# Strassen-like down projection of an MLP on one core: weight sums formed in place, a seventh buffer of split weights, first-step weights ahead of the last four u tiles, relu and square on ScalarE

## The chip, the cores and the metric

The kernel runs on one core of one Trainium2 chip. Its time is the device time of one execution in microseconds (us); before the change it is 2210.37 us, the median of three runs (2208.81, 2210.37, 2213.05). Engines are named as the profile names them: PE is TensorE (matmuls), PEld its weight load, DVE VectorE, ACT ScalarE, POOL GpSimd, SP SyncE, which issues the loads.

## The reference, cut to what matters

Two layers, 256 tokens, model width 2048, hidden width 8192, everything in float32. The change touches the MLP, the last line of a layer.

```python
for l in range(DEPTH):
    h = rmsnorm(x, attn_norm[l])
    proj = h @ w_in[l]
    ...                                     # latent attention (a) and retention (r)
    x = x + mixed @ w_o[l]
    h = rmsnorm(x, mlp_norm[l])
    x = x + jnp.square(jax.nn.relu(h @ w_up[l])) @ w_down[l]
return rmsnorm(x, final_norm)
```

## The kernel before, in words

**Weights.** All weights come as float32 from DRAM, one load per piece (`w_load`, L124, on SP's queue), into five raw buffers (N_RAW) of 4 KB a partition. Each raw piece is split into a rounded head, cast on ACT (L189), and a tail, raw minus head, on DVE (L190); head and tail stand in one of six `w` buffers (N_SPLIT). A product with a split operand is then two matmuls: 512 columns (weight head times activation head and tail, `mac_feat`, L223) and 256 columns (weight tail times activation head, L224). These two are called a pair below. `proj_feat` runs one output tile or four of them in PSUM banks of their own, and `join` (an ACT copy, L241, and a DVE add, L242) brings a bank's two halves together.

**The MLP.** A layer's hidden width is worked off in four blocks of 2048 (FB). A block first makes 16 tiles u0 to u15 of squared-relu activations, in four groups of four tiles: four PSUM banks a group, eight in all. Of each tile, join gives t; then t = max(t, 0) * t in one DVE instruction (L759), t times the row scale `rs2b` (L760), and the split into u, head on ACT (L182) and tail on DVE (L183). Each pair of tiles gives a step's combined activations f0 to f7 (`first_factors`, L684 to L687).

The down projection of a block has two parts. Columns 0 to 767 of w_down go through eight steps of `seven_products`: seven products of 3 matmuls of 384 columns each (L724), a Strassen-like scheme of 2 by 2 tiles that keeps seven PSUM banks over the whole block. Its weight operands come from `second_factors`: two loads of 128x768, casts of w11 alone (384 columns) and of w21 and w22 together (768), then four DVE adds into two further buffers of the raw pool (L707, L708, L710, L711), which are cast and split in their turn (768 each). The other columns are done as ordinary tiles: behind nearly every step stands `next_tile` (two loads of 128x8x128, 16 pairs, a join, and an add into x, L777). In a layer's last block a tile stands behind six of the eight steps, and every finished tile goes on into the next norm (`done_x`: L185, L186, L266, L267). A block ends with `gather_products`, which takes the seven banks into SBUF (ACT copies in a layer's first block, DVE adds, L732, in the others). A layer ends with `join_products` (DVE, L738) and the tiles left.

**Order.** The program is built in the order of the Python code, and a scheduler then fixes one order for each engine. Each engine works its own list in order: an instruction that waits holds up what stands behind it on the same engine. The eighth PSUM bank is the only one free while the seven product banks are held, and the raw and `w` buffers are handed round in order.

Of the kernel before, what the change touches and what calls it, by code (L numbers as in the profile page):

```python
# [11 lines left out]
F32 = mybir.dt.float32  # L12
# [28 lines left out]
N_RAW, N_SPLIT = 5, 6  # L41
# [52 lines left out]
def kernel(ctx: ExitStack, tc: tile.TileContext, xt, positions, w_in, w_uq, w_ukv, w_o, w_up, w_down,  # L94
# [35 lines left out]
    for j in range(0, KD, 2):  # L130
# [4 lines left out]
        if j == 8:  # L135
            cst = cpool.tile([P, C_W], F32, name="cst")
            nc.sync.dma_start(cst, consts)
            posi = cpool.tile([P, T], I32, name="posi")
            nc.sync.dma_start(posi, positions.to_broadcast([P, T]))
# [12 lines left out]
    angles = cpool.tile([P, 2, 2, T], F32, tag="tabs", name="angles")  # L152
    turn = cpool.tile([P, T], F32, tag="rsb", name="turn")
    ang, part, k2 = tab[:, 0, 0, :], tab[:, 0, 1, :], tab[:, 1, 0, :]
    ks = [k2, turn, k2]
    nc.gpsimd.tensor_copy(turn, posi)
    nc.gpsimd.tensor_scalar_mul(ang, turn, cst[:, C_FREQ:C_FREQ + 1])
    for k, (turns, parts) in zip(ks, REDUCTIONS):
        nc.gpsimd.tensor_scalar(k, ang, 1.0 / (2 * math.pi * turns), ROUND, op0=ALU.mult, op1=ALU.add)
        for n, size in parts:  # L160
            nc.gpsimd.tensor_scalar(part, ks[n], -ROUND, size, op0=ALU.add, op1=ALU.mult)
            nc.gpsimd.tensor_tensor(ang, ang, part, op=ALU.subtract)
    nc.gpsimd.tensor_scalar(ang, ang, PI_LOW, -PI_LOW, op0=ALU.min, op1=ALU.max)
    for i in range(2):
        nc.gpsimd.tensor_copy(angles[0:64, i, 0, :], ang[i * 64:i * 64 + 64, :])
        nc.gpsimd.tensor_scalar_mul(angles[64:128, i, 0, :], ang[i * 64:i * 64 + 64, :], -1.0)

    def rotary_tables():
        for i in range(2):
            ang, half = angles[:, i, 0, :], angles[:, i, 1, :]  # L170
# [141 lines left out]
    def spread(c, tag=None):  # L312
# [6 lines left out]
        d = cpool.tile([P, T], F32, tag=tag, name=tag)  # L319
# [25 lines left out]
    for l in range(DEPTH):  # L345
        g0 = l * G_LAYER

        with tc.tile_pool(name=f"mix{l}", bufs=1) as ap:
            mixed = [None] * 16

# [40 lines left out]
            def scale_rows():  # L391
# [16 lines left out]
                rows["rsb"] = spread(rows["rs"], "rsb")  # L408
                rows["tkvb"] = spread(rows["tkv"], "tkvb")
                rows["tabs"] = tabs = cpool.tile([P, 2, 2, T], F32, tag="tabs", name="tabs")  # L410
# [195 lines left out]
            def mix_latent():  # L606
# [5 lines left out]
                ta = spread(rc, "tab_a")  # L612
# [36 lines left out]
        with tc.tile_pool(name=f"mlp{l}", bufs=1) as up:  # L649
# [195 lines left out]
```

## Time and profile before

| | |
|---|---|
| runs | 2208.81, 2210.37, 2213.05 us |
| profiled execution | 2210.41 us, span 2208.6 us |
| PE busy | 2159.2 us, 98% of the span |
| DVE busy | 1794.2 us, 81% |
| ACT busy | 1219.0 us, 55% |
| mixer and w_o, layer 1 | to about 355 us |
| eight-step stages, first matmul of L724 | 471.3, 649.9, 827.9, 1005.3 us (layer 1); 1559.9, 1738.5, 1916.1, 2094.8 us (layer 2) |
| eight-step stages, last matmul of L724 | 543.5, 721.7, 899.1, 1074.9 us; 1632.1, 1809.9, 1988.5, 2164.8 us |

A busy share of PE counts matmuls whose ends are modelled, so the pace is better read from the starts of successive matmuls. In a list of instructions each row gives start, busy time, engine, line, operation, and in brackets the idle time of the engine just before it with what ended it.

### The profile page before, as it was taken

Reading aid. Unit: us, or ns where it says so; the run is one execution under the profiler, and the core shown is the slowest. Engines: PE = TensorE matmul, PEld = TensorE weight load, DVE = VectorE, ACT = ScalarE, POOL = GpSimd, SP = SyncE. Lnnn points to the kernel's source line nnn. Section 1 sums busy time; section 2 is a strip of 40 time slices with the busy share of each in tenths; the row PEclk is TensorE's granted clock in tenths of the full one; section 3 lists DMA queues with packets and bytes.
Section 4 is the critical chain, followed back from the end, with each engine's and each line's share of the span. In section 5 each row is a group of like instructions: output and inputs, shape, how many; then the busy total and the mean of one; then the engine's idle time right before and its main releaser. Section 6 shows DMA issues by size and latency. Waiting matters only on the chain.

```text
span 2208.6 us, 33675 instructions
## 1 busy us (share of the span) xinstructions
PE 2159.2 (98%) x12398; PEld 1910.3 (86%) x12398; DVE 1794.2 (81%) x3451; ACT 1219.0 (55%) x1976; POOL 24.5 (1%) x34
## 2 busy tenths in 40 slices
PE   7999999999999999999999999999999999999997
PEld 6888888888888888888898888888888898888876
DVE  8878967788688779788978888668887887887787
ACT  7555546556555555555655554555565555555554
POOL 4000000000000000000000000000000000000000
PEclk9999999999999999999999999999999999999999
DMA  7555556547737755854765555565586476467454
GB/s 244 167 157 177 161 190 186 179 137 218 220 123 201 233 166 168 251 158 148 219 177 154 176 164 168 179 196 167 147 250 188 127 229 210 133 194 236 152 168 128
DMA packets 367845, 400.15 MB, mean 181 GB/s; under 512 B 13120, under 2 KB 271296, under 8 KB 367680
## 3 DMA queue, kind: packets, MB, share of 16 engines
q1 hardware_dynamic: 366720, 397.08, 59.9%
q8 instruction: 97, 1.59, 0.3%
q10 hardware_dynamic: 960, 0.92, 0.1%
q14 instruction: 68, 0.56, 0.1%
HBM read 395.85 MB, written 2.10 MB: 180 GB/s over the span
## 4 chain that ended last, share of the span: by engine, by line
PE 78%; DVE 12%; DMA 6%; ACT 2%; issue 1%; SPq 0%; ACTq 0%; DVEq 0%
PE mm L223 42%; PE mm L224 22%; DMA raw<-w_down 6%; DVE w L190 5%; PE mm L228 3%; PE mm L724 3%; ACT w L189 2%; PE mm L229 1%; PE at L223 1%; DVE raw L708 1%; PE at L224 1%; DVE t L242 1%; DVE raw L710 1%; DVE raw L707 1%; PE at L492 0%
## 5 line engine op out<-in xcount | busy, mean ns | idle before, releaser
L190 DVE TENSOR_TENSOR w<-raw,w 128x1024 fp32r<-128x1024 f32 (+5 forms) x952 | 1014.9, 1077 | 324.9 <-ACT w L189 320.0
L189 ACT CAST w<-raw 128x1024 fp32r<-128x1024 f32 (+5 forms) x952 | 877.7, 933 | 666.7 <-PE mm L224 420.2
L223 PE MATMUL mm<-xs,w 128*128 128x512 f32 x2944 | 1032.6, 394 | 7.7 <-ACT w L189 7.7
L224 PE MATMUL mm<-xs,w 128*128 128x256 f32 x2944 | 826.9, 281 | 4.9 <-DVE w L190 4.9
L223 PEld LDWEIGHTS mm<-xs,w 128*128 128x128 f32 x2944 | 553.2, 188 | 126.4 <-ACT w L189 8.0
L224 PEld LDWEIGHTS mm<-xs,w 128*128 128x128 f32 x2944 | 555.1, 189 | 7.4 <-DVE w L190 7.1
L223 PE MATMUL mm<-u,w 128*128 128x512 f32 x1280 | 452.5, 393 | 5.8 <-ACT w L189 5.8
L224 PE MATMUL mm<-u,w 128*128 128x256 f32 x1280 | 365.5, 286 | 7.7 <-DVE w L190 7.6
L223 PEld LDWEIGHTS mm<-u,w 128*128 128x128 f32 x1280 | 241.7, 189 | 54.8 <-ACT w L189 6.9
L224 PEld LDWEIGHTS mm<-u,w 128*128 128x128 f32 x1280 | 242.5, 189 | 21.5 <-DVE w L190 21.0
L223 PE MATMUL mm<-mix,w 128*128 128x512 f32 x512 | 178.0, 391 | 0.0
L241 ACT COPY tb<-mm 128x256 f32<-128x256 f32 x296 | 106.4, 372 | 122.1 <-PE mm L224 118.2
L724 PE MATMUL mm<-w,f 128*128 128x384 f32 x768 | 155.3, 342 | 4.4 <-ACT w L189 2.5
L724 PEld LDWEIGHTS mm<-w,f 128*128 128x128 f32 x768 | 132.1, 188 | 15.6 <-DVE w L190 7.3
L224 PE MATMUL mm<-mix,w 128*128 128x256 f32 x512 | 143.7, 281 | 0.0
L242 DVE TENSOR_TENSOR t<-mm,tb 128x256 f32<-128x256 f32 x296 | 116.9, 417 | 29.9 <-ACT tb L241 28.9
L724 PE MATMUL mm<-w,u 128*128 128x384 f32 x576 | 127.7, 340 | 9.1 <-DVE t L242 7.6
L223 PEld LDWEIGHTS mm<-mix,w 128*128 128x128 f32 x512 | 96.1, 188 | 20.8
L724 PEld LDWEIGHTS mm<-w,u 128*128 128x128 f32 x576 | 98.8, 188 | 17.1 <-issue 9.9
L182 ACT CAST f<-t 128x256 fp32r<-128x256 f32 x128 | 52.1, 407 | 83.3 <-DVE t L687 44.4
L224 PEld LDWEIGHTS mm<-mix,w 128*128 128x128 f32 x512 | 96.4, 188 | 0.0
L228 PE MATMUL mm<-w,xs 128*128 128x512 f32 x256 | 92.8, 401 | 0.0
(196 smaller groups left out, 1716.0 us busy)
## 6 DMA issues: line engine op xcount, KB each, us to landing
raw<-w_up SPq DMA_DIRECT2D x256, 512.0 KB, 4.5
raw<-w_down SPq DMA_DIRECT2D x160, 512.0 KB, 4.2
raw<-w_in SPq DMA_DIRECT2D x144, 512.0 KB, 4.5
raw<-w_down SPq DMA_DIRECT2D x128, 384.0 KB, 4.9
raw<-w_o SPq DMA_DIRECT2D x64, 512.0 KB, 4.5
raw<-w_uq SPq DMA_DIRECT2D x16, 384.0 KB, 4.1
raw<-w_in SPq DMA_DIRECT2D x16, 320.0 KB, 3.3
raw<-w_ukv SPq DMA_DIRECT2D x8, 512.0 KB, 4.3
```

Source lines behind the costliest of these rows:

```text
L182: nc.scalar.copy(head, src)
L189: nc.scalar.copy(dst_h, src)
L190: nc.vector.tensor_tensor(dst_l, src, dst_h.bitcast(F32), op=ALU.subtract)
L223: nc.tensor.matmul(ps, wk[:, 0, n0:n0 + P], act.rearrange("p s t -> p (s t)"), start=first, stop=False)
L224: nc.tensor.matmul(ps[:, 0:T], wk[:, 1, n0:n0 + P], act[:, 0, :], start=False, stop=last)
L228: nc.tensor.matmul(ps, act[:, 0, t0:t0 + P], wk, start=first, stop=False)
L229: nc.tensor.matmul(ps[:, 0:256], act[:, 1, t0:t0 + P], wk[:, 0], start=False, stop=last)
L241: nc.scalar.copy(tb, ps[:, T:2 * T])
L242: nc.vector.tensor_tensor(dst, ps[:, 0:T], tb, op=ALU.add)
L707: nc.vector.tensor_tensor(sums[0][:, 0, :], w11, w12, op=ALU.add)
L708: nc.vector.tensor_tensor(sums[0][:, 1, :], w22, w12, op=ALU.add)
L724: nc.tensor.matmul(ps[i], a[:, p, :], w[:, q, :], start=first and n == 0, stop=last and n == 2)
```

## The change

Five edits, of which the core of the diff follows. (1) `second_factors` forms its four sums in the two raw buffers themselves, after the casts of w11, w21 and w22 have been taken from them, and so takes two buffers of the raw pool a step instead of four; the last two of its operands change places. (2) There are seven `w` buffers instead of six. Room for it comes from moving some rotary and row-scale tiles into a pool that is open only during the mixer (not shown). (3) In every block the weights of the first step are called for before the joins of the last four u tiles; of these tiles, join and relu come for all four, and the rest (square, row scale, split) stands in the code behind the first step's products, f6 and f7 behind the first two tiles. (4) Relu and square are two ACT instructions in place of one on DVE. (5) At the end of a layer one tile is called for between `gather_products` and `join_products`.

```diff
-N_RAW, N_SPLIT = 5, 6
+N_RAW, N_SPLIT = 5, 7
...
                 parts([w11], w11)
                 parts([w21, w22], raws[1])
-                sums = [wpool.tile([P, 2, SB], F32, tag="raw", name="raw", bufs=N_RAW) for _ in range(2)]
-                nc.vector.tensor_tensor(sums[0][:, 0, :], w11, w12, op=ALU.add)
-                nc.vector.tensor_tensor(sums[0][:, 1, :], w22, w12, op=ALU.add)
-                parts("13", sums[0].rearrange("p i c -> p (i c)"))
-                nc.vector.tensor_tensor(sums[1][:, 0, :], sums[0][:, 0, :], w22, op=ALU.add)
-                nc.vector.tensor_tensor(sums[1][:, 1, :], sums[1][:, 0, :], w21, op=ALU.add)
-                parts("24", sums[1].rearrange("p i c -> p (i c)"))
+                for dst, other in ((w11, w12), (w12, w22), (w22, w11), (w21, w22)):
+                    nc.vector.tensor_tensor(dst, dst, other, op=ALU.add)
+                parts([w11, w12], raws[0])
+                parts([w21, w22], raws[1])
...
-                        join(ps, t)
-                        nc.vector.scalar_tensor_tensor(t, t, 0.0, t, op0=ALU.max, op1=ALU.mult)
-                        nc.vector.tensor_tensor(t, t, rows["rs2b"], op=ALU.mult)
...
+                def next_u(t):
+                    nc.scalar.activation(t, t, AF.Square)
+                    nc.vector.tensor_tensor(t, t, rows["rs2b"], op=ALU.mult)
...
+                def relu_sum(ps):
+                    t = tmp()
+                    join(ps, t)
+                    nc.scalar.activation(t, t, AF.Relu)
+                    return t
...
+                factors = second_factors(b * FB)
+                late = [relu_sum(ps) for ps in pss]
...
-                for k, f in enumerate(fs):
-                    seven_products(pp, us, f, k, b * FB + 2 * k * P, k == 0, k == len(fs) - 1)
+                steps = FB // (2 * P)
+                for k in range(steps):
+                    if k:
+                        factors = second_factors(b * FB + 2 * k * P)
+                    seven_products(pp, us, fs[k], k, factors, k == 0, k == steps - 1)
+                    while late:
+                        next_u(late.pop(0))
                     if k in (LAST_TILE_AFTER if end else TILE_AFTER):
                         next_tile()
+                    if pair:
+                        next_f()
                 gather_products(pp, sums, b == 0)
                 if end:
+                    next_tile()
                     blocks = join_products(sums)
```

Where the change moves instructions, the scheduled lists show. On ACT, where the first block's up phase passes into its steps, the list before reads as follows; `tb` are the copies of the last four u tiles' banks, `w` of 384 and 768 columns belong to step weights and those of 8x128 to a tile.

```order
L189 CAST w_5121<-raw_5117 128x384
L182 CAST f5_4869<-t_4871 128x256
L189 CAST w_5124<-raw_5119 128x768
L189 CAST w_5131<-raw_5127 128x768
L189 CAST w_5136<-raw_5128 128x768
L189 CAST w_5163<-raw_5161 128x8x128
L241 COPY tb_5053<-mm_4880 128x256
L241 COPY tb_5062<-mm_4881 128x256
L241 COPY tb_5082<-mm_4882 128x256
L241 COPY tb_5091<-mm_4883 128x256
L189 CAST w_5184<-raw_5182 128x8x128
L189 CAST w_5212<-raw_5208 128x384
```

The same place on ACT now, from the last copies of the banks on:

```order
L246 COPY tb_5100<-mm_4895 128x256
L776 ACTIVATE t_5089<-t_5089 128x256
L776 ACTIVATE t_5094<-t_5094 128x256
L776 ACTIVATE t_5099<-t_5099 128x256
L762 ACTIVATE t_5084<-t_5084 128x256
L762 ACTIVATE t_5089<-t_5089 128x256
L762 ACTIVATE t_5094<-t_5094 128x256
L187 CAST u12_5134<-t_5084 128x256
L187 CAST u13_5139<-t_5089 128x256
L187 CAST u14_5144<-t_5094 128x256
L762 ACTIVATE t_5099<-t_5099 128x256
L194 CAST w_5215<-raw_5211 128x384
```

The first step's weight casts stood ahead of the four bank copies already and still do; the cast of the first tile's second half has moved ahead of the copies too. New behind the copies are relu (L776) and square (L762) of four tiles. The second step's first two weight casts (w_5215, and w_5218 right behind it) stand ahead of the cast of u15.

On DVE at the same place, before, from the join of tile 12 on (the L190 row is the tail of the first tile's second half, L685 to L687 belong to f6):

```order
L242 TENSOR_TENSOR t_5052<-mm_4880,tb_5053 128x256
L242 TENSOR_TENSOR t_5061<-mm_4881,tb_5062 128x256
L759 SCALAR_TENSOR_TENSOR t_5052<-t_5052 128x256
L759 SCALAR_TENSOR_TENSOR t_5061<-t_5061 128x256
L760 TENSOR_TENSOR t_5052<-t_5052,rs2b_4276 128x256
L760 TENSOR_TENSOR t_5061<-t_5061,rs2b_4276 128x256
L685 TENSOR_TENSOR t_5071<-t_5052 128x128
L684 TENSOR_TENSOR t_5071<-t_5052,t_5061 128x128
L190 TENSOR_TENSOR w_5184<-raw_5182,w_5184 128x8x128
L183 TENSOR_TENSOR u12_5058<-t_5052,u12_5058 128x256
L183 TENSOR_TENSOR u13_5067<-t_5061,u13_5067 128x256
L686 TENSOR_TENSOR t_5072<-t_5071,t_5052 128x128
```

The same place on DVE now, from the tail of the first tile's second half on:

```order
L195 TENSOR_TENSOR w_5176<-raw_5174,w_5176 128x8x128
L247 TENSOR_TENSOR t_5084<-mm_4892,tb_5085 128x256
L247 TENSOR_TENSOR t_5089<-mm_4893,tb_5090 128x256
L247 TENSOR_TENSOR t_5094<-mm_4894,tb_5095 128x256
L247 TENSOR_TENSOR t_5099<-mm_4895,tb_5100 128x256
L763 TENSOR_TENSOR t_5084<-t_5084,rs2b_4276 128x256
L763 TENSOR_TENSOR t_5089<-t_5089,rs2b_4276 128x256
L763 TENSOR_TENSOR t_5094<-t_5094,rs2b_4276 128x256
L188 TENSOR_TENSOR u12_5134<-t_5084,u12_5134 128x256
L188 TENSOR_TENSOR u13_5139<-t_5089,u13_5139 128x256
L188 TENSOR_TENSOR u14_5144<-t_5094,u14_5144 128x256
L763 TENSOR_TENSOR t_5099<-t_5099,rs2b_4276 128x256
```

Before, twelve instructions (the ten rows above from the first L759 on, and two more) stood between the first two joins and the last two; now the four joins follow one another, the weight tail stands ahead of them, and f6 has gone behind the first tile.

On DVE at the end of the first layer, before (L732 are the gathers, L738 the joining of products, w_11081 and w_11102 the halves of the next tile's weights):

```order
L732 TENSOR_TENSOR p6_5855<-p6_5855,mm_10396 128x384
L732 TENSOR_TENSOR p4_5857<-p4_5857,mm_10397 128x384
L738 TENSOR_TENSOR p2_5847<-p1_5845,p2_5847 128x384
L738 TENSOR_TENSOR p6_5855<-p1_5845,p6_5855 128x384
L190 TENSOR_TENSOR w_11081<-raw_11079,w_11081 128x8x128
L738 TENSOR_TENSOR p7_5853<-p6_5855,p7_5853 128x384
L190 TENSOR_TENSOR w_11102<-raw_11100,w_11102 128x8x128
L738 TENSOR_TENSOR p4_5857<-p7_5853,p4_5857 128x384
```

The same place now:

```order
L737 TENSOR_TENSOR p6_5855<-p6_5855,mm_10390 128x384
L737 TENSOR_TENSOR p4_5857<-p4_5857,mm_10391 128x384
L195 TENSOR_TENSOR w_11074<-raw_11072,w_11074 128x8x128
L195 TENSOR_TENSOR w_11095<-raw_11093,w_11095 128x8x128
L743 TENSOR_TENSOR p2_5847<-p1_5845,p2_5847 128x384
L743 TENSOR_TENSOR p6_5855<-p1_5845,p6_5855 128x384
L195 TENSOR_TENSOR w_11135<-raw_11133,w_11135 128x8x128
L743 TENSOR_TENSOR p7_5853<-p6_5855,p7_5853 128x384
```

The next tile's two tails have moved ahead of two and three joining adds, and are still behind the seven gathers.

## Rows read from the trace of the kernel before

**Rows 1.** Page, part 1: busy us (share of span) xinstructions.
```profile
PE 2159.2 (98%) x12398; PEld 1910.3 (86%) x12398; DVE 1794.2 (81%) x3451; ACT 1219.0 (55%) x1976; POOL 24.5 (1%) x34
```

**Rows 2.** Busy time by window: PE, PEld, DVE, ACT, POOL, then clock, DMA share.
```profile
400.00:420.00 20.00, 20.00 (x118) 17.64 (x117) 16.62 (x36) 11.88 (x20) 0.00 (x0) 1.00 0.56 168
460.00:480.00 20.00, 18.87 (x108) 16.60 (x107) 16.56 (x39) 9.54 (x18) 0.00 (x0) 1.00 0.39 118
```

**Rows 3.** Matmuls of L724 in block 1 and block 4 of layer 1.
```profile
L724 PE MATMUL mm<-w,u x72: 333/338/440, 471.3 to 543.5; 128*128 128x384 f32 x72
...
L724 PE MATMUL mm<-w,u x72: 334/337/448, 1005.3 to 1074.9; 128*128 128x384 f32 x72
```

**Rows 4.** PE's instructions in order, start of block 1's first step.
```profile
471.31 1.21 PE L724 MATMUL mm<-w,u 128*128 128x384 f32 x6
472.36 2.24 PE L724 MATMUL mm<-w,f 128*128 128x384 f32 x12
474.44 0.34 PE L724 MATMUL mm<-w,u 128*128 128x384 f32 x1
474.96 0.44 PE L724 MATMUL mm<-w,u 128*128 128x384 f32 x1 [0.18 <-ACT w L189]
475.23 0.34 PE L724 MATMUL mm<-w,f 128*128 128x384 f32 x1
476.52 0.76 PE L724 MATMUL mm<-w,u 128*128 128x384 f32 x3 [0.95 <-DVE t L242]
```

**Rows 5.** DVE's instructions in order, the same stretch of block 1.
```profile
475.96 0.74 DVE L242 TENSOR_TENSOR t<-mm,tb 128x256 f32<-128x256 f32 x2
...
476.96 0.75 DVE L759 SCALAR_TENSOR_TENSOR t<-t 128x256 f32<-128x256 f32 x2
```

**Rows 6.** PE's instructions in order, second step and its tile.
```profile
486.35 0.39 PE L223 MATMUL mm<-u,w 128*128 128x512 f32 x1
487.01 0.39 PE L224 MATMUL mm<-u,w 128*128 128x256 f32 x1 [0.28 <-DVE w L190]
487.24 0.39 PE L223 MATMUL mm<-u,w 128*128 128x512 f32 x1
...
487.58 0.39 PE L223 MATMUL mm<-u,w 128*128 128x512 f32 x1
```

**Rows 7.** ACT's waits, steps of block 1, 500 to 540 us: us, times, longest.
```profile
ACT w L189 <- DMA raw<-w_down: 9.5, 10, 2.0
```

**Rows 8.** Busy time by window, block 4 of layer 1 (columns as in Rows 2).
```profile
1005.28:1075.23 69.95, 65.74 (x363) 57.98 (x361) 65.23 (x118) 42.26 (x68) 0.00 (x0) 1.00 0.56 163
```

**Rows 9.** PE's instructions in order, end of block 1.
```profile
543.71 0.40 PE L223 MATMUL mm<-u,w 128*128 128x512 f32 x1
544.54 0.39 PE L224 MATMUL mm<-u,w 128*128 128x256 f32 x1 [0.43 <-DVE w L190]
```

**Rows 10.** PE's instructions in order, end of layer 1's steps.
```profile
1075.07 0.40 PE L223 MATMUL mm<-u,w 128*128 128x512 f32 x1
1078.63 0.50 PE L223 MATMUL mm<-u,w 128*128 128x512 f32 x1 [3.17 <-ACT w L189]
1080.13 0.58 PE L224 MATMUL mm<-u,w 128*128 128x256 f32 x1 [1.00 <-DVE w L190]
...
1083.49 0.39 PE L223 MATMUL mm<-u,w 128*128 128x512 f32 x1
```

**Rows 11.** ACT's instructions in order, end of layer 1's steps.
```profile
1077.53 1.04 ACT L189 CAST w<-raw 128x1024 fp32r<-128x1024 f32 x1 [0.78 <-DMA raw<-w_down]
```

**Rows 12.** PE's instructions in order, end of layer 2's steps.
```profile
2164.95 0.40 PE L223 MATMUL mm<-u,w 128*128 128x512 f32 x1
2167.63 0.50 PE L223 MATMUL mm<-u,w 128*128 128x512 f32 x1 [2.28 <-ACT w L189]
```

**Rows 13.** ACT's instructions in order, block 1's last four tiles.
```profile
470.47 1.41 ACT L241 COPY tb<-mm 128x256 f32<-128x256 f32 x4 [0.64 <-PE mm L224]
```

**Rows 14.** Groups of ACT instructions: count | busy us, mean ns | idle before.
```profile
L266 ACT ACTIVATE sq<-x 128x256 f32<-128x256 f32 x74 | 29.4, 406 | 10.7 <-DVE ssq L267 6.7 <-DVE x L777 3.9
```

More of the change, by code (lines that the diff above doesn't have):

```diff
@@ L137 @@
             nc.sync.dma_start(cst, consts)
-            posi = cpool.tile([P, T], I32, name="posi")
+            posi = cpool.tile([P, T], I32, tag="rs2b", name="posi")
             nc.sync.dma_start(posi, positions.to_broadcast([P, T]))
@@ L151, with rotary_angles @@
     tab = cpool.tile([P, 2, 2, T], F32, name="tab")
[L152 to L166, printed above, removed]
+    angles = []
+    def rotary_angles(pool):
+        angle = pool.tile([P, 2, 2, T], F32, tag="tabs", name="angles")
+        angles.append(angle)
+        turn = pool.tile([P, T], F32, tag="rsb", name="turn")
+        ang, part, k2 = tab[:, 0, 0, :], tab[:, 0, 1, :], tab[:, 1, 0, :]
+        ks = [k2, turn, k2]
+        nc.gpsimd.tensor_copy(turn, posi)
+        nc.gpsimd.tensor_scalar_mul(ang, turn, cst[:, C_FREQ:C_FREQ + 1])
+        for k, (turns, parts) in zip(ks, REDUCTIONS):
+            nc.gpsimd.tensor_scalar(k, ang, 1.0 / (2 * math.pi * turns), ROUND, op0=ALU.mult, op1=ALU.add)
+            for n, size in parts:
+                nc.gpsimd.tensor_scalar(part, ks[n], -ROUND, size, op0=ALU.add, op1=ALU.mult)
+                nc.gpsimd.tensor_tensor(ang, ang, part, op=ALU.subtract)
+        nc.gpsimd.tensor_scalar(ang, ang, PI_LOW, -PI_LOW, op0=ALU.min, op1=ALU.max)
+        for i in range(2):
+            nc.gpsimd.tensor_copy(angle[0:64, i, 0, :], ang[i * 64:i * 64 + 64, :])
+            nc.gpsimd.tensor_scalar_mul(angle[64:128, i, 0, :], ang[i * 64:i * 64 + 64, :], -1.0)
     def rotary_tables():
         for i in range(2):
-            ang, half = angles[:, i, 0, :], angles[:, i, 1, :]
+            ang, half = angles[0][:, i, 0, :], angles[0][:, i, 1, :]
             nc.scalar.activation(half, ang, AF.Sin, scale=0.5)
@@ L310, in norm_col, with spread @@
         return rsqrt(v, 2)
-    def spread(c, tag=None):
+    def spread(c, tag=None, pool=cpool):
         ps = abank()
@@ L318, in spread @@
             return ps[:, 0:T]
-        d = cpool.tile([P, T], F32, tag=tag, name=tag)
+        d = pool.tile([P, T], F32, tag=tag, name=tag)
         nc.scalar.copy(d, ps[:, 0:T])
@@ L349 @@
             mixed = [None] * 16
+            if l == 0:
+                rotary_angles(ap)
             def two(tag, bufs=1):
@@ L407, in scale_rows @@
                     yield
-                rows["rsb"] = spread(rows["rs"], "rsb")
-                rows["tkvb"] = spread(rows["tkv"], "tkvb")
-                rows["tabs"] = tabs = cpool.tile([P, 2, 2, T], F32, tag="tabs", name="tabs")
+                rows["rsb"] = spread(rows["rs"], "rsb", ap)
+                rows["tkvb"] = spread(rows["tkv"], "tkvb", ap)
+                rows["tabs"] = tabs = ap.tile([P, 2, 2, T], F32, tag="tabs", name="tabs")
                 for i in range(2):
```

32 lines of the change are left out of this document (18 added, 14 removed).

## The prediction

> **What bounds the kernel now.** The busy times come first: PE is busy for 98% of the span, DVE for 81%, ACT for 55% [rows 1]. A PE at 98% looks as if nothing were left, but a matmul's end is modelled, so the next thing to read is the pace from start to start. In a stretch without a wait, one matmul of 384 columns follows another after (472.36 − 471.31)/6 = 0.174 us [rows 4], and a pair (512 and 256 columns) after 487.58 − 487.24 = 0.34 [rows 6], 0.347 us in the mean over undisturbed stretches; per matmul both are 0.174 us. In a window of the up phase PE starts 118 matmuls and is never idle; in the window that holds the passage from the up phase to the first step it starts 108 and is idle for 1.1 us [rows 2]. The kernel is therefore bound by PE, except where the steps begin, run and end.
>
> How much that is: a normal block has 8 steps of 21 matmuls and 7 tiles of 16 pairs from its first to its last matmul of L724, at full pace 167 × 0.174 + 112 × 0.347 = 67.9 us from first start to last. Block 1 takes 543.5 − 471.3 = 72.2 [rows 3]; the six normal blocks (three a layer) lie between 71.3 and 72.4, mean 71.9, by the same kind of row: excess 4.0 each. A last block has six tiles in the stretch, 62.4 us at full pace, and takes 69.6 [rows 3], the other 70.0: excess 7.4 each.
>
> The instructions in order say where this goes. At a block's start PE loses 0.35 us at 474.44, 0.10 at 474.96 and 1.29 − 0.17 = 1.12 at 475.23, 1.6 in all. The three single rows from 474.44 on are matmuls of the second step that the scheduler had put ahead of the first step's seventh product; the seventh product itself, at 476.52, waits for a DVE join [rows 4], because the bank that it needs still holds one of the last two u tiles, and their joins come only at 475.96, after other DVE work [rows 5]. In the second step PE waits for a weight tail: 0.66 instead of 0.23 us at 486.35 [rows 6]; summed over all its matmuls the second step loses 1.0. Later the loads are late: from 500 to 540 us ACT's casts wait 9.5 us in ten waits for raw data [rows 7]. After a block's last step, PE loses 0.83 − 0.23 = 0.6 us [rows 9]. At layer 1's end it loses 3.56 − 0.23 = 3.33 and 1.50 − 0.23 = 1.27 us [rows 10]; ACT there waits for raw data [rows 11]. Then five pairs take 3.36 us at the lower clock, some 1.6 too much. Layer 2's end loses 2.68 − 0.23 = 2.45 in the same way [rows 12], and 1.3 and 1.4 behind it. Together: starts 8 × 1.6 = 12.8, rest of six normal blocks 6 × 2.4 = 14.4, rest of two last blocks 2 × 5.8 = 11.6, block ends 6 × 0.6 = 3.6, layer ends 6.2 + 5.2 = 11.4: 53.8 us within reach, and no part of the change touches the mixers' PE work.
>
> **The change part by part.** *Four joins in a row.* Two joins take 0.74 us, 0.33 apart from start to start [rows 5], so the four joins take some 1.4 us behind the first copy, and the banks of the late tiles are free before the fifth product, the first that needs one of them, 12 × 0.174 = 2.1 us after the up phase's last matmul, and well before the seventh, 3.1 us after it. PE's list now has no matmul of the second step inside the first. The 1.12 goes and most of the rest; I leave 0.2 a block: −8 × 1.4 = −11.2. What is late next is u15, which the first tile needs as the last of its 16 inputs, 21 × 0.174 + 15 × 0.347 = 8.9 us after the up phase. On ACT stand ahead of it four copies, four relus, four squares, four casts and two weight casts. Four copies in a row took 1.41 us, 0.35 apart [rows 13]; a square in its own takes 0.41 [rows 14]. So 16 × 0.35 + 1.35 = 7.0 us packed, 16 × 0.41 + 1.35 = 7.9 unpacked, plus 0.4 for the tail on DVE: 7.4 to 8.3 against 8.9. I take the packed value and no cost; the margin is 0.6 to 1.5 us.
>
> *Relu and square on ACT.* 128 DVE instructions of 0.33 us go (−43 us of DVE), and 256 ACT instructions of at least 0.35 come (+90 us of ACT, from 55% to 59%). In the up phase ACT is busy 11.9 of 20 us and DVE 16.6 [rows 2], and PE waits for neither: nothing there, either way.
>
> The Trainium skill, "ScalarE: Activation LUTs", section "Rules for kernel authors", says to put relu on VectorE and not on ScalarE, since VectorE is up to three times faster per element in bf16. The rows here, float32 in 256 columns, show nearly one price for an instruction on either engine, 0.33 and 0.35 us apart in a row; by the rule the edit would be a loss, and it speaks for the slower rival below, by the rows it costs nothing while u15 keeps its margin.
>
> *Sums in place and the seventh buffer.* A step and its tile take four buffers of the raw pool instead of six, out of five, so a load can start about half a step earlier. The waits for loads were 9.5 us in 40, about 2.2 in the 9.2 us of a step and its tile. The adds keep their number and size, but each now needs the tail of the operand that it overwrites, and two more depend on the one before. In the normal blocks DVE has room. I let the second step's 1.0 us go and a third of the remaining 1.4: −6 × 1.5 = −9.0; bounds 0 and −14.4. In the last blocks DVE itself is nearly the bound: it is busy for 65.2 of 69.95 us [rows 8], the change takes only 4 × 0.33 = 1.3 from that, and 63.9 us is more than PE's 62.4. Starts aside, at most 69.6 − 1.4 − 63.9 = 4.3 can go in each; I take half: −2 × 2.3 = −4.6; bounds 0 and −8.6.
>
> *Block and layer ends.* The tail that PE waits for after the last step comes sooner with a seventh buffer: −1.5 of 3.6, bounds 0 and −3.6. At a layer's end the two weight tails of the next tile move ahead of two or three of the joining adds, 1 to 1.4 us, but still stand behind seven gathers, and the raw buffer for the tile after it is free only when the last step's tails are done, so the load remains late: −3.5 of 11.4, bounds +2 and −11.4 (if the gap becomes short enough, the clock stays at 2.4 GHz and 3.0 of these go by themselves).
>
> Sum: −11.2 − 9.0 − 4.6 − 1.5 − 3.5 = −29.8. The profiled execution took 2210.41 us, the median of the runs is 2210.37: 2180.6, say 2181 us. All that the bounds give: −12.8 − 14.4 − 8.6 − 3.6 − 11.4 = −51, 2159 us.
>
> **The rivals.** *DVE and the loads stay the bound.* The same joins, scalings and tails have to be done behind the up phase, and the adds in place make a longer chain. If the starts give only half (−5.6), the rest of the normal blocks a third (−5), ends as forecast (−5) and the last blocks nothing: −15.6, 2195 us. For it: DVE's 65.2 of 69.95. Against it: over the span DVE is busy for 81% only [rows 1], and the normal blocks have none of the last blocks' work for the next norm.
>
> *Everything goes:* 2160 us. For it: most waits come from order and buffers, not from work. Against it: the last blocks' DVE and the gathers.
>
> *The change does nothing much.* The scheduler had the first step's weight casts ahead of the last copies already, so this edit is in effect before; and PE is at 98%. Then only the long join wait halves: −8 × 0.5, 2206 us. Against it: the rows give the wait's name, and the joins do move.
>
> *Slower: u15 comes late.* ACT works in order, and the second step's two weight casts stand ahead of u15's cast. If their loads land late, because the raw buffer is held longer by the sums in place, u15 waits behind them, and PE, with the tile ahead of the second step, stands still. The other terms give −18.6, so this decides once a start loses over 1.6 + 18.6/8 = 3.9 us. At 5 us a block: +8 × 3.4 − 18.6 = +8.6, 2219 us. Against it: the margin of 0.6 to 1.5 us, and that the first of these raw buffers is free before the up phase ends.
>
> **How the numbers follow.** Forecast 2181 (2172 to 2192 by itself): 0.55. DVE and loads, 2195: 0.17. Everything, 2160: 0.12. Nothing much, 2206: 0.08, a quarter of it below the bound. Slower, 2219: 0.08. Some 0.2%, 4.4 us, is what a measurement of this kernel can tell from no change: faster 0.55 + 0.17 + 0.12 + 0.02 = 0.86, same 0.06, slower 0.08. Leaving out the far half of "everything" and the slower case, the range is 2161 to 2200.
>
> **What would show it.** Right: no wait of L729 (the seven products' line) for a DVE join in the first step; first to last matmul of a normal block near 69, of a last block near 66; a gap of 3 to 5 us left at the layer ends. Wrong: the pairs with u12 to u15 in the first tile waiting for ACT or DVE; ACT's casts waiting as long for raw data as now; the first step's own products waiting for their casts; or a pace of 0.174 us that has changed by itself, which would move the time in stretches that the change doesn't touch.

## The result and the profile after

The changed kernel takes 2179.99 us (median of four runs, 2177.83 to 2180.52) against 2210.86 of the kernel before beside it: a ratio of 0.9858, 95% interval 0.9841 to 0.9875. The forecast was 2181 us. The profiled execution took 2180.52 us, its span is 2178.7 where it was 2208.6: 29.9 us less, against a sum of 29.8. The total was met; several of its terms were not, and their errors cancelled, as the places below show.

The page's busy times, answering to [rows 1]:

```profile
PE 2145.7 (98%) x12398; PEld 1918.1 (88%) x12398; DVE 1768.0 (81%) x3323; ACT 1274.9 (59%) x2232; POOL 24.4 (1%) x34
```

PE still reads 98%. DVE has 128 instructions less and ACT 256 more, as counted. The busy share does not show a gain of 30 us; the starts do. PE's instructions in order at block 1's first step, answering to [rows 4]:

```profile
471.43 1.21 PE L729 MATMUL mm<-w,u 128*128 128x384 f32 x6
472.48 2.24 PE L729 MATMUL mm<-w,f 128*128 128x384 f32 x12
474.56 0.68 PE L729 MATMUL mm<-w,u 128*128 128x384 f32 x3
475.07 0.40 PE L228 MATMUL mm<-u,w 128*128 128x512 f32 x1
475.31 0.28 PE L229 MATMUL mm<-u,w 128*128 128x256 f32 x1
```

No bracket is left: 21 matmuls in 3.64 us, and the tile follows at once. The waits of ACT between 500 and 540 us, answering to [rows 7] (us, times, longest):

```profile
ACT w L194 <- DVE raw L715: 8.9, 7, 2.7
...
ACT w L194 <- DMA raw<-w_down: 2.1, 3, 1.1
```

The wait for loads has fallen from 9.5 us to 2.1, and a wait for the adds, 8.9 us, stands in its place. What it costs PE the experiments show. What is left in a normal block is mainly one short wait in the third step's tile, as in block 1 (block 2 of layer 1 loses 0.7 us more than the others):

```profile
493.50 0.40 PE L228 MATMUL mm<-u,w 128*128 128x512 f32 x1
494.25 0.39 PE L229 MATMUL mm<-u,w 128*128 128x256 f32 x1 [0.36 <-DVE w L195]
```

The seven products' matmuls of blocks 1 and 4 of layer 1, first and last start at the end of a row, answering to [rows 3]:

```profile
L729 PE MATMUL mm<-w,u x72: 333/337/345, 471.4 to 540.1; 128*128 128x384 f32 x72
...
L729 PE MATMUL mm<-w,u x72: 333/337/522, 995.4 to 1063.5; 128*128 128x384 f32 x72
```

Block 1 takes 68.6 us (72.2 before, 67.9 at full pace), block 4 takes 68.1 (69.6 before, 62.4 at full pace). In block 4 most of the loss lies in the fifth step. PE's instructions there:

```profile
1029.17 0.51 PE L729 MATMUL mm<-w,f 128*128 128x384 f32 x2
1031.42 0.62 PE L729 MATMUL mm<-w,f 128*128 128x384 f32 x2 [1.75 <-ACT w L194]
1032.63 1.14 PE L729 MATMUL mm<-w,f 128*128 128x384 f32 x5 [0.59 <-ACT w L194]
```

And two windows of that block (columns as in rows 2). In the first DVE has no free time to speak of; in the second, just behind the waits, the granted clock (third figure from the right) is 0.50:

```profile
1010.00:1035.00 25.00, 21.91 (x119) 19.52 (x118) 24.47 (x44) 14.70 (x24) 0.00 (x0) 0.97 0.51 151
1033.64:1037.05 3.41, 3.41 (x12) 3.12 (x11) 3.39 (x4) 2.08 (x3) 0.00 (x0) 0.50 0.81 255
```

Layer 2's last block waits 1.13 and 0.62 us at the same place, keeps its clock, and takes 65.5 us.

The end of layer 1's steps, answering to [rows 10]:

```profile
1063.71 0.63 PE L228 MATMUL mm<-u,w 128*128 128x512 f32 x2
1067.54 0.61 PE L228 MATMUL mm<-u,w 128*128 128x512 f32 x1 [3.19 <-ACT w L194]
1067.94 0.41 PE L229 MATMUL mm<-u,w 128*128 128x256 f32 x1
```

ACT waits there for raw data as it did in [rows 11], and pairs from 1067.94 on take 0.64 us again, at the lower clock:

```profile
1066.44 1.04 ACT L194 CAST w<-raw 128x1024 fp32r<-128x1024 f32 x1 [0.61 <-DMA raw<-w_down]
```

```profile
1067.77:1071.19 3.42, 3.42 (x12) 2.84 (x12) 3.42 (x6) 0.00 (x0) 0.00 (x0) 0.50 0.70 202
```

Where the 29.9 us came from, by stretches of the two traces (sums over the layers; "forecast" regroups the terms of the prediction by these stretches, a start's 1.4 included):

| stretch | before | after | change | forecast |
|---|---|---|---|---|
| six normal blocks, first to last matmul of the seven products | 431.4 | 412.8 | −18.6 | −17.4 |
| two last blocks, the same | 139.6 | 133.6 | −6.0 | −7.4 |
| six passages from a normal block's last step to the next first step | 637.5 | 634.5 | −3.0 | −1.5 |
| layer 1's last step to layer 2's first step | 485.0 | 484.0 | −1.0 | |
| layer 2's last step to the end | 43.8 | 42.4 | −1.4 | |
| both of these together | 528.8 | 526.4 | −2.5 | −3.5 |
| start to the first step | 471.3 | 471.4 | +0.1 | 0 |

### The profile page after: what moved, and what is told of

Read it like the earlier page. It is cut to its first block, busy times and chain, and to the rows that moved or that the text cites. A ratio compares the mean times of both kernels' runs of the same rounds, so it can differ in the third digit from the quotient of the medians.

```text
span 2178.7 us, 33827 instructions
## 1 busy us (share of the span) xinstructions
PE 2145.7 (98%) x12398; PEld 1918.1 (88%) x12398; DVE 1768.0 (81%) x3323; ACT 1274.9 (59%) x2232; POOL 24.4 (1%) x34
## 4 chain that ended last, share of the span: by engine, by line
PE 83%; DVE 10%; ACT 3%; issue 2%; DMA 2%; SPq 0%; ACTq 0%; DVEq 0%
PE mm L228 44%; PE mm L229 23%; PE mm L729 5%; DVE w L195 4%; PE mm L233 3%; DVE raw L715 3%; PE mm L234 1%; PE at L228 1%; ACT w L194 1%; DMA raw<-w_down 1%; PE at L229 1%; DVE t L763 1%; ACT tb L246 1%; PE at L498 0%; PE at L499 0%
## 5 line engine op out<-in xcount | busy, mean ns | idle before, releaser
L195 DVE TENSOR_TENSOR w<-raw,w 128x1024 fp32r<-128x1024 f32 (+4 forms) x952 | 1013.0, 1077 | 308.0 <-ACT w L194 298.9
L729 PE MATMUL mm<-w,f 128*128 128x384 f32 x768 | 145.8, 337 | 4.1 <-ACT w L194 4.1
L715 DVE TENSOR_TENSOR raw<-raw 128x384 f32<-128x384 f32 x256 | 142.4, 556 | 6.6
L729 PE MATMUL mm<-w,u 128*128 128x384 f32 x576 | 122.4, 338 | 0.0
```

What stands on the lines that cost most here:

```text
L195: nc.vector.tensor_tensor(dst_l, src, dst_h.bitcast(F32), op=ALU.subtract)
L715: nc.vector.tensor_tensor(dst, dst, other, op=ALU.add)
L729: nc.tensor.matmul(ps[i], a[:, p, :], w[:, q, :], start=first and n == 0, stop=last and n == 2)
```

## The experiments

Each kernel was timed over five rounds beside the kernel before, whose medians were 2209.68, 2210.11 and 2209.99 us in the three series. "Changed" below means the changed kernel, 2179.99 us, ratio 0.9858. It was timed beside a median of 2210.86, about 1 us above those three, so a difference to it in us is uncertain by about that much; where it matters, the difference of the ratios is given too. Stretches are those of one profiled execution each.

**One part taken back.** First the late part (3): all four groups of u tiles are treated alike, and the first step's weights are called for at the first step.

```diff
-                for c in range(0, FB - UP_TILES * P, UP_TILES * P):
+                for c in range(0, FB, UP_TILES * P):
...
-                pss = proj_feat(w_up[l], 0, (b + 1) * FB - UP_TILES * P, ms, UP_TILES)
-                factors = second_factors(b * FB)
-                late = [relu_sum(ps) for ps in pss]
...
-                    if k:
-                        factors = second_factors(b * FB + 2 * k * P)
+                    factors = second_factors(b * FB + 2 * k * P)
...
-                    while late:
-                        next_u(late.pop(0))
...
-                    if pair:
-                        next_f()
```

> The changed kernel with the late part alone taken back: the last four u tiles are each joined, squared, scaled and split before the first step's weights are called for, as in the kernel before. Theory (the joins of four tiles in a row free the banks): the first step's seventh product waits for a DVE join again, 1.1 us and 0.5 more around it, and the second step's weights come late, so each of the eight block starts loses 1.6 to 2.6 us more: 8 x 1.6 to 8 x 2.4 = 13 to 19 us, 2193 to 2199 us. Rival (the scheduler settles the order anyway, and buffers and in-place sums made the gain): under 4 us, at most 2184. If it is the buffers that matter at the start, no wait of L729 for a DVE join is seen in the first step.

Measured: 2185.61 us, ratio 0.9890 (0.9875 to 0.9905), 5.6 us above changed (7.1 by the ratios), under the range and above the rival's limit. The wait is back, as PE's row in block 1 shows:

```profile
474.40 0.85 PE L729 MATMUL mm<-w,u 128*128 128x384 f32 x4
475.10 0.34 PE L729 MATMUL mm<-w,f 128*128 128x384 f32 x1
476.62 0.76 PE L729 MATMUL mm<-w,u 128*128 128x384 f32 x3 [1.19 <-DVE t L247]
```

and DVE's list shows why: two joins, eleven other instructions, then the other two joins.

```profile
470.92 0.75 DVE L247 TENSOR_TENSOR t<-mm,tb 128x256 f32<-128x256 f32 x2
...
476.06 0.75 DVE L247 TENSOR_TENSOR t<-mm,tb 128x256 f32<-128x256 f32 x2
```

The six normal blocks take 70.0 to 70.1 us each instead of 68.6 to 69.4, 7.7 more together. The last blocks take what they took in changed (68.2 and 65.5), though the wait at their start is back too. What is lost at the start there is not lost later: in block 4 the third step's tile no longer waits its 0.75 us, and the wait of 1.75 us in the fifth step falls to 1.07. Some 2.4 us come back behind layer 2's last step. The mechanism holds, the gain in the last blocks doesn't.

Next, relu and square back on DVE (4).

```diff
-                    nc.scalar.activation(t, t, AF.Square)
+                    nc.vector.scalar_tensor_tensor(t, t, 0.0, t, op0=ALU.max, op1=ALU.mult)
...
-                    nc.scalar.activation(t, t, AF.Relu)
```

> The changed kernel with relu and square back in one DVE instruction, all else kept. Theory: the edit is worth nothing in the up phase, and at block starts DVE has 4 x 0.33 us more, ACT 8 x 0.35 less: 0 to +4 us, 2179 to 2184. Rival one (a rule that keeps relu on VectorE holds): faster than the changed kernel by 2 us or more, since u12 to u15 no longer pass over ACT three times each. Rival two (DVE is the bound in the last blocks and at the starts): slower by over 5 us, with the last blocks' first-to-last stretch longer by over 1.3 us each.

Measured: 2177.23 us, ratio 0.9852 (0.9837 to 0.9867), 2.8 us below changed by the medians, 1.3 by the ratios, with intervals that overlap. The normal blocks take 68.6 to 68.8 us, 0.6 less together, all of it in block 2 of layer 1; the last ones take 68.1 and 65.7, though DVE is busy about 1 us longer in each (65.6 us of block 4 instead of 64.6). Of the profiled difference of 3.5 us, 2.6 lie behind layer 2's last step (39.8 us to the end instead of 42.4): changed has waits of 0.61 and 1.02 us there and a spell at the lower clock from 2142.97, this kernel 0.31 and 0.25 and no such spell. The kernel without the late part, whose relu and square are on ACT, takes 40.0 there, so that stretch doesn't hang on this edit alone. The time leans to the first rival, but its mechanism, tiles u12 to u15 coming earlier, is not what moved. In changed, u15's tail is taken from 476.92 to 477.34, 5.9 us after the up phase, and PE needs it 8.9 us after.

Six buffers of split weights instead of seven (2).

```diff
-N_RAW, N_SPLIT = 5, 7
+N_RAW, N_SPLIT = 5, 6
```

> The changed kernel with six instead of seven buffers of split weights. Theory: the seventh buffer lets ACT cast one piece further ahead, which shows at block ends and in the second tile half after a step: +2 to +8 us, 2182 to 2188, with 0.3 to 0.6 us back at each block end and in the second step. Rival (ACT waits mostly for PE to free a buffer in the up phase, 404 us in the changed kernel, where it costs nothing; in the steps the casts wait for raw data or sums): within 2 us of 2180.

Measured: 2188.38 us, ratio 0.9902 (0.9885 to 0.9919), 8.4 us above changed (9.7 by the ratios), just beyond the theory's range: the largest of the single losses. It does not lie at the block ends, whose passages take 105.7 us as in changed, but in the steps: 69.8 to 70.1 us in the normal blocks, 69.2 and 66.8 in the last. In block 1 the second step waits for a cast, and for a tail:

```profile
482.58 0.40 PE L228 MATMUL mm<-u,w 128*128 128x512 f32 x1
483.38 0.61 PE L729 MATMUL mm<-w,f 128*128 128x384 f32 x2 [0.41 <-DVE w L195]
483.83 0.68 PE L729 MATMUL mm<-w,u 128*128 128x384 f32 x3
485.09 0.44 PE L729 MATMUL mm<-w,u 128*128 128x384 f32 x1 [0.57 <-ACT w L194]
```

Four pieces belong to a step and two to its tile, so with six buffers none is left for a seventh piece until one is released. At the first step this shows on ACT: in changed the first tile's second half is cast ahead of the bank copies, 2.6 us before the first product, and with six buffers behind them, 3.8 us after it (first products at 471.43 and 470.27). First changed, then six buffers:

```profile
468.85 1.05 ACT L194 CAST w<-raw 128x1024 fp32r<-128x1024 f32 x1 [1.73 <-PE mm L229]
```

```profile
474.11 1.04 ACT L194 CAST w<-raw 128x1024 fp32r<-128x1024 f32 x1
```

The sums in two raw buffers of their own again (1).

```diff
-                for dst, other in ((w11, w12), (w12, w22), (w22, w11), (w21, w22)):
-                    nc.vector.tensor_tensor(dst, dst, other, op=ALU.add)
-                parts([w11, w12], raws[0])
-                parts([w21, w22], raws[1])
+                sums = [wpool.tile([P, 2, SB], F32, tag="raw", name="raw", bufs=N_RAW) for _ in range(2)]
...
+                parts("13", sums[0].rearrange("p i c -> p (i c)"))
...
+                parts("24", sums[1].rearrange("p i c -> p (i c)"))
```

> The changed kernel with the four sums again in two further buffers of the raw pool, all else kept. Theory (four of five raw buffers a step instead of six let the loads start earlier): ACT's wait for loads of w_down goes back from 36 towards 125 us, the normal blocks lose 1 to 2.4 us each and the layer ends 1 to 2: +8 to +18 us, 2188 to 2198. Rival (the in-place adds cost as much as they give: in the changed kernel ACT waits 175 us for the adds): within 4 us of 2180, or faster in the last blocks, where the adds in place hold DVE and ACT in turn.

Measured: 2184.18 us, ratio 0.9884 (0.9869 to 0.9899), 4.2 us above changed (5.7 by the ratios), between theory and rival. ACT's waits for w_down loads go back to 113.6 us, but the normal blocks don't lose (68.1 to 69.3 us). The passages do: 106.2 to 106.6 us instead of 105.7 to 105.8, 3.6 together. PE's rows at the end of block 1, answering to [rows 9]:

```profile
540.21 0.40 PE L228 MATMUL mm<-u,w 128*128 128x512 f32 x1
541.13 0.38 PE L229 MATMUL mm<-u,w 128*128 128x256 f32 x1 [0.52 <-DVE w L195]
```

In changed this wait is gone (pairs of 0.35 us from 540.24 on). So it is the sums in place that cure the block ends, and the seventh buffer that cures the steps; the prediction had them the other way round. The table behind the next three experiments bears this out.

The tile between gathering and joining at the layer ends, left out (5).

```diff
                 if end:
-                    next_tile()
                     blocks = join_products(sums)
```

> The changed kernel without the one tile between gathering and joining at the layer ends. Theory (that tile's weight tails then go back among the joining adds on DVE, 1 to 1.4 us later, while PE waits for them): +1 to +4 us over the two layers, 2181 to 2184. Rival (PE waits for the loads of the tiles behind, not for these tails): within 1 us of 2180.

Measured: 2179.05 us, ratio 0.9859 (0.9844 to 0.9874): no difference. The stretch from layer 1's last step to layer 2's first takes 1.1 us more, and layer 2's last block and what follows it 1.6 less. This edit is worth nothing in the whole that these runs can tell.

**One part alone.** Each of three edits by itself on the kernel before: sums in place; the seventh buffer; the late part. These are the diffs above, read the other way, one at a time.

> Of the changes only the sums in place: six buffers of split weights, u tiles in the old order, relu and square on DVE, no tile between gather and join. With it taken from the changed kernel the time rose by 4.2 us. Theory (parts overlap: each takes away some of the same waits, so one alone gives more than its loss when taken back from all): 5 to 12 us below the kernel before, 2198 to 2205, with the wait of ACT for w_down loads falling from 125 us to about 40. Rival (parts add up): 4 us below, 2206.

> Of the changes only the seventh buffer of split weights. With it taken from the changed kernel the time rose by 8.4 us. Theory (without the sums in place the casts in the steps wait for loads, which a further buffer behind them doesn't hasten): less than its loss, 2 to 6 us below the kernel before, 2204 to 2208. Rival (parts add up): 8 us below, 2202.

> Of the changes only the late part: the first step's weights called for before the last four joins, square, scale and split of these tiles behind the first step's products, f6 and f7 behind the first two tiles; relu and square in one DVE instruction. Theory (the four joins in a row free the banks, which has nothing to do with buffers): the 1.6 us at each block start go, and some of the second step's 1.0: 10 to 18 us below the kernel before, 2192 to 2200. Rival (parts add up, 5.6 us): 2204. If the second step then waits for its own weights in place of the join, the gain is under 5 us.

| part | alone: time, ratio | alone, against before | taken back from changed |
|---|---|---|---|
| sums in place | 2194.92, 0.9934 (0.9920 to 0.9947) | −15.2 | +4.2 |
| seventh buffer | 2192.74, 0.9921 (0.9909 to 0.9934) | −17.4 | +8.4 |
| late part | 2196.59, 0.9938 (0.9926 to 0.9951) | −13.5 | +5.6 |

Alone the three give 46.1 us, and all together with the other two edits 30.9 (33 with relu and square on DVE). So they overlap: by these medians about half or more of what each gives alone is not missed when it alone is taken back. The theory of overlap held in kind for the sums in place, though their 15.2 lie above its 5 to 12, and for the late part, at 13.5; it failed for the seventh buffer, which I thought would be idle behind late loads: it gave 17.4, beyond its rival too, with ACT's wait for loads still at 104.6 us. With it the normal blocks take 69.3 to 70.0 us though the sums stand apart, and in the first step only 0.35 and 0.40 us are left as single waits. With the late part alone the first step's seventh product waits for nothing; the second step's tile then loses 0.74 us at a DVE tail.

The traces hold all eight combinations of the three parts (us, summed over both layers; "loads" is ACT's wait for loads of w_down):

| buffers, sums, late part | six normal blocks | six passages | loads |
|---|---|---|---|
| six, apart, no (before) | 431.4 | 637.5 | 124.8 |
| six, in place, no | 428.1 | 634.1 | 35.7 |
| seven, apart, no | 417.4 | 637.6 | 104.6 |
| seven, in place, no | 420.4 | 634.3 | 25.1 |
| six, apart, yes | 419.6 | 637.8 | 98.4 |
| six, in place, yes | 419.4 | 634.1 | 25.0 |
| seven, apart, yes | 412.1 | 638.1 | 113.6 |
| seven, in place, yes (changed) | 412.8 | 634.5 | 36.2 |

The sums in place take 3.3 to 3.7 us from the passages whatever the rest, and move the normal blocks by −3.3, +3.0, −0.2 and +0.7, though they take 73 to 89 us from the wait for loads each time. The seventh buffer takes 6.6 to 14.0 us from the normal blocks and nothing from the passages; the late part takes 5.3 to 11.8 from the normal blocks, least where the seventh buffer stands beside it. (The four kernels that lack at most one of the three parts have the two other edits, the rest don't; taken back, these moved the normal blocks by 0.6 and 0.1 and the passages not at all.)

**What is left, and a better version.** The first kernel has relu and square on DVE and calls for the layer-end tile ahead of the gathering.

```diff
-                gather_products(pp, sums, b == 0)
                 if end:
                     next_tile()
+                gather_products(pp, sums, b == 0)
+                if end:
                     blocks = join_products(sums)
```

> The changed kernel with relu and square back on DVE, and at a layer's end the one tile called for ahead of the gathering of the seven products, where the changed kernel has it between gathering and joining. On DVE the tile's two weight tails then stand behind one or two gathers in place of seven, and on PE no matmul of the tiles after it stands inside it. Theory (at the layer ends PE waits first for these tails and for the loads of the tiles after): of the 3.4 and 1.6 us lost at layer 1's end in the changed kernel, and 0.8, 1.3 and 1.5 at layer 2's, two thirds go: 4 to 7 us below the 2177 of the kernel with relu and square on DVE, 2170 to 2173. Rival (the load itself is late, since its raw buffer is freed by the last step's tails): under 2 us.

Measured: 2176.41 us, ratio 0.9848 (0.9834 to 0.9861). That is 0.8 us below the 2177.23 of the kernel it was built on, so the rival's "under 2" holds in sum. The wait at layer 1's end is broken up rather than removed: DVE takes both tails before six of the seven gathers,

```profile
1060.43 1.22 DVE L195 TENSOR_TENSOR w<-raw,w 128x1024 fp32r<-128x1024 f32 x1
...
1061.90 1.22 DVE L195 TENSOR_TENSOR w<-raw,w 128x1024 fp32r<-128x1024 f32 x1
1063.03 0.55 DVE L737 TENSOR_TENSOR p<-p,mm 128x384 f32<-128x384 f32 x1
```

the tile runs through without the 3.2 us wait, and PE waits afterwards, for tails and joining adds, at 1069.50, 1073.56 and 1074.69:

```profile
1069.50 0.39 PE L229 MATMUL mm<-u,w 128*128 128x256 f32 x1 [0.97 <-DVE w L195]
...
1073.56 0.88 PE L752 MATMUL at<-cst,p 128*128 128x128 f32 x6 [0.67 <-DVE p L743]
1074.69 0.38 PE L229 MATMUL mm<-u,w 128*128 128x256 f32 x1 [0.26 <-DVE w L195]
```

The clock does not fall at this end. From layer 1's last step to layer 2's first the stretch is 1.8 us shorter, and behind layer 2's last step 0.9 longer.

On this kernel, the adds into x and into the sum of squares of the last block's tiles 6 to 11 were given to GpSimd.

```diff
-            nc.vector.tensor_tensor(acc, acc, sq, op=ALU.add)
+            (eng or nc.vector).tensor_tensor(acc, acc, sq, op=ALU.add)
...
-                    add_square(acc_n, x[j], not squared)
+                    add_square(acc_n, x[j], not squared, nc.gpsimd if j < 12 else None)
...
-                    nc.vector.tensor_tensor(x[j], x[j], t, op=ALU.add)
+                    (nc.gpsimd if end and j < 12 else nc.vector).tensor_tensor(x[j], x[j], t, op=ALU.add)
```

> The kernel with relu and square on DVE and the tile ahead of the gathering, with the adds into x and into the sum of squares of the last block's tiles 6 to 11 on GpSimd instead of DVE. Theory (in a layer's last block DVE is the bound: it is busy 24.5 of 25 us where the fourth and fifth step lose 2.7 us): 6 x 0.67 us go from DVE in each last block, and its stretch falls from 68.0 and 65.7 towards 65 and 64: 2 to 5 us below 2176.4. Rival (not DVE's work but its order and the steps without a tile set the loss): no change in the stretches beyond 0.5 us. Against both: GpSimd may slow DVE where both work on the same memory, then DVE's instructions in the last blocks get longer than 0.42 us for 256 columns and the time rises.

Measured: 2181.26 us, ratio 0.9868 (0.9854 to 0.9883), 4.9 us slower; the last blocks take 69.5 and 68.4 us instead of 68.0 and 65.7. GpSimd's rows beside DVE's:

```profile
1016.63 0.74 POOL L796 TENSOR_TENSOR x<-x,t 128x256 f32<-128x256 f32 x1 [9.63 <-DVE t L247]
1018.29 1.15 POOL L272 TENSOR_TENSOR ssq<-ssq,sq 128x256 f32<-128x256 f32 x1 [0.93 <-ACT sq L271]
```

```profile
1016.47 0.28 DVE L691 TENSOR_TENSOR t<-t 128x128 f32<-128x128 f32 x1
1016.67 0.85 DVE L692 TENSOR_TENSOR t<-t 128x128 f32<-128x128 f32 x1
1017.44 0.28 DVE L693 TENSOR_TENSOR t<-t 128x128 f32<-128x128 f32 x1
1017.64 1.21 DVE L195 TENSOR_TENSOR w<-raw,w 128x1024 fp32r<-128x1024 f32 x1
1018.78 0.95 DVE L191 SCALAR_TENSOR_TENSOR xs<-x,gain,xs 128x256 fp32r<-128x256 f32 x1
```

A DVE instruction of 0.28 us takes 0.85 while GpSimd adds, one of 0.48 takes 0.95. DVE gets back nothing of the 0.33 that it gave away: in block 4 it is busy for 65.6 us as before, with 12 instructions fewer. The condition put against both theories is what happened.

The other cure: a tile behind each of the first seven steps of the last blocks.

```diff
-TILE_AFTER, LAST_TILE_AFTER = range(8), (0, 1, 2, 4, 5, 6)
+TILE_AFTER, LAST_TILE_AFTER = range(8), range(7)
```

> The kernel with relu and square on DVE and the tile ahead of the gathering, with a tile behind each of the first seven steps of a layer's last block instead of six of eight, so that no step in the middle is without one. Theory (the loss at the fifth step of the last blocks, 1.9 + 0.75 us and after it 1.5 at the lower clock in layer 1, 1.3 + 0.8 in layer 2, comes because the fourth step has no tile: PE reaches the next step after 3.65 us, DVE needs 4.9 for its weights): most of it goes, 3 to 6 us below 2176.4, 2170 to 2173. Rival (the loss moves to the layer's end, where one tile less is left to cover the gathering and joining): within 2 us of 2176.4.

> Both together: a tile behind each of the first seven steps of the last blocks, and the adds of tiles 6 to 11 on GpSimd. Theory (two cures of one loss): not below the better of the two alone by more than 2 us. Rival (DVE's whole work bounds the last block as well): below it by 2 us or more.

Measured: 2176.22 us, ratio 0.9847 (0.9832 to 0.9861), and with GpSimd's adds 2178.75, 0.9858 (0.9841 to 0.9874). With seven tiles the waits at the fifth step are gone in both layers: the last blocks take 69.6 and 69.0 us with a tile more in them, where full pace is 67.9. A tile counted at 16 × 0.347 = 5.6 us, layer 1 wins 3.9 in the block. That comes back at layer 1's end, 5.7 longer by the same count, where fewer tiles cover the joining adds and the tails:

```profile
1075.69 0.55 PE L752 MATMUL at<-cst,p 128*128 128x128 f32 x3 [0.55 <-DVE p L743]
1077.82 1.02 PE L752 MATMUL at<-cst,p 128*128 128x128 f32 x6 [1.59 <-DVE p L743]
1086.67 0.38 PE L229 MATMUL mm<-u,w 128*128 128x256 f32 x1 [3.13 <-DVE w L195]
```

So the rival holds for the whole time and for layer 1, where the loss moved; in layer 2 it did not move, 2.2 us are won in the block and 1.1 more behind it. With both cures the kernel is 2.5 us slower than with seven tiles alone: the last blocks take 73.5 and 71.5 us. The best versions, 2176.2 to 2176.4 us, are 3.6 to 3.8 us below the changed kernel by their medians and 2.2 to 2.4 by the ratios; their intervals overlap with its own, so a gain over it is likely but not settled.

## Why the prediction was right, point by point

That the sum came within 1 us of the measured time is luck. By its terms the late part was 3.5 us too large and the layer ends 1.0, buffers and sums were 3.4 too small and the rest of the last blocks 1.4, and these errors cancel. The mechanism was right in part.

- **What bounds the kernel.** Reading starts of matmuls, not busy shares, put 53.8 us within reach in the steps and ends, and all of the gain came from there: the stretch ahead of the first step moved by 0.1 us. Confirmed.
- **Four joins in a row, −11.2.** Within the changed kernel the late part is worth 7.7 us in the six normal blocks, 1.3 each where 1.4 was forecast. In the last two blocks it is worth nothing, because the time won at their start is waited away in the third and fifth steps. The term was 3.5 us too large, mostly for that reason. By itself on the kernel before, the part gives more, 13.5 us, because it also does some of the seventh buffer's work: in the normal blocks 11.8 without that buffer and 5.3 with it, the sums apart both times.
- **u15.** Its tail came 5.9 us after the up phase, not 7.4 to 8.3: the first copy began before the up phase's last matmul, and three relus took 1.04 us, 0.31 apart where 0.35 was reckoned. The margin is 3.0 us, and the slower rival never came near.
- **Relu and square on ACT at nothing.** By the blocks' stretches this is right to 0.2 us in seven of the eight; in block 2 of layer 1 the edit costs 0.7. Taken back, the whole time fell by 1.3 to 2.8 us, mostly at another place, and the runs don't settle whether the edit is the cause. By the Trainium skill, "ScalarE: Activation LUTs", section "Rules for kernel authors", the edit is the wrong way round. The sign agrees, within overlapping intervals; no run shows the rule's reason at work, and on these rows an instruction costs nearly the same on both engines.
- **Sums in place and the seventh buffer, −9.0 and −1.5.** The sum, 10.5, stands against 13.9 to explain (18.6 − 7.7 in the normal blocks and 3.0 in the passages), but each went to the wrong place. The sums in place were to cure the steps by earlier loads; undone, they bring back the waits for loads and cost the steps nothing. The seventh buffer was to cure the block ends; undone, it costs the steps 6.7 us in the normal blocks and 2.4 in the last, and the ends nothing. The failed step is that a wait of ACT for a load was taken as a wait of PE. ACT's wait for loads can go from 36 to 114 us with seven buffers, and from 25 to 98 with six, while the six normal blocks together stay the same to 0.7 us.
- **Last blocks, −7.4 with their starts.** Measured −6.0. DVE's work there, 64.6 us busy in block 4 where 63.9 was reckoned, is more than PE's 62.4 and so a floor, as argued. It is not the whole reason: relu and square on DVE added about 1 us to it and left the block's 68.1 as they were. What I had not seen is that the loss gathers behind the one step in the middle without a tile, and that in layer 1 a spell at the lower clock follows.
- **Layer ends, −3.5.** Measured −2.5, of which 1.0 at layer 1's end, and the tile between gathering and joining can account for that: without it the stretch is 1.1 us longer. The 1.4 at layer 2's end are not this edit's; without it that end is shorter still. The gathers ahead of the tails and the late loads are as argued; moved, the wait turns up at the joining adds.

Of the signs named beforehand, the join's wait is gone and the normal blocks are near 69 us; the last blocks are at 68.1 and 65.5 where 66 was named, and a gap of 3 to 5 us is left at layer 1's end only (3.19), against 0.61 and 1.02 at layer 2's.

What stays open: why the stretch behind layer 2's last step varies between 39 and 45 us among the kernels with six tiles in the last blocks. Those with a spell at the lower clock near its start take 42.3 to 45.2, those without 39.1 to 41.6, and the waits at its start add up to between 0.3 and 3.3 us; what sets these waits was not tried. Open too is what less work for DVE would give in the last blocks: the one attempt, GpSimd's adds, did not lessen DVE's time.

## What to carry to other kernels

Measure what a stall costs on the engine that bounds the kernel, by starts of its instructions against its undisturbed pace; the longest wait in the table may be one that a buffer hides. When several edits give slack to one chain, take each back from the whole as well as trying it alone: alone they gave 46 us here, together 31, and without any one of them 21 to 26. Look at each stretch by itself as well: a part can give the same everywhere, as the sums in place at the block ends, or only where another part is missing. Where one engine is nearly full, as DVE in the last blocks, a change of order can move a loss to the next place where that engine is short (layer 1) or remove it (layer 2).

## What the runs showed of the hardware

GpSimd's adds in SBUF lengthen the DVE instructions that run beside them: 128x128 subtractions in float32 from 0.28 to 0.85 us, a 128x256 scaling from 0.48 to 0.95, while GpSimd's own adds of 128x256 took 0.74 to 1.65 us in layer 1's last block. In the rows shown the one that begins second is the longer one: DVE's tail at 1017.64, begun before GpSimd's add at 1018.29, keeps its 1.21 us, and that add takes 1.15 where the shortest took 0.74.

A wait of 3.2 us of PE at layer 1's end was followed by pairs at 0.64 us instead of 0.35, at a granted clock of 0.5, that is 1.2 GHz, from 1067.77 to 1071.19 us; in the kernel whose waits there were all under 1 us this did not happen. The length of one wait does not decide it: with the sums in place alone PE waited 3.16 us at the same place, and with seven tiles 3.13 us at 1086.67, and pairs behind both took 0.35 us at a granted clock of 1.00:

```profile
1076.09:1079.91 3.82, 3.82 (x24) 3.38 (x24) 3.82 (x7) 0.09 (x1) 0.00 (x0) 1.00 0.59 167
1086.67:1092.00 5.33, 5.33 (x31) 4.70 (x32) 5.33 (x9) 2.62 (x5) 0.00 (x0) 1.00 0.64 169
```
